# Index relu written in PSUM instead of SBUF, pieces of vector work on other engines, and the mixer's steps in another order

## The chip, the cores and the metric

The kernel runs on one core of one Trainium2 chip, with its inputs and its output in the chip's memory. The metric is the device time of one execution in microseconds (us), lower being better. Engines are called TensorE (PE in the profile), VectorE (DVE), ScalarE (ACT), GpSimd (POOL) and SyncE (SP, which here issues transfers).

## The reference

One decoder layer on 512 tokens of width 1024 in float32: a feed-forward block (FFN1), a token mixer, a second feed-forward block (FFN2). The mixer's group A selects keys with an indexer, then attends to them; group B is a latent attention over all earlier keys.

```python
x = x + 0.5 * swiglu(rmsnorm(x), gate1, up1, down1)          # D_FF = 2816
p = rmsnorm(x) @ W_in                                        # columns split among the groups
# group A, for each block i of 128 queries
idx_logits = einsum('bqhd,bsd->bqhs', q_idx, k_idx)          # 16 index heads of width 64
score = einsum('bqh,bqhs->bqs', w_idx, relu(idx_logits))
_, sel = top_k(where(causal, score, -inf), 128)              # 128 keys per query
att = softmax(q . k[sel]) @ v[sel]                           # 8 heads share one key and value
# group B: 8 heads, q and kv through normalised latents, dense causal softmax
x = x + concat(out_A, out_B) @ W_out
x = x + 0.5 * swiglu(rmsnorm(x), gate2, up2, down2)
```

## The kernel before

Every product of a projection is made in three matmuls of split operands (high times high, high times low, low times high; `mm3`, L137, L140 and L141). The split of a weight piece is a copy on ScalarE (L94) and a subtraction on VectorE or GpSimd (L95). FFN1 runs until 395 us of the span, the mixer until 691 us, then FFN2.

The mixer's order is a table, `ORDER`, of steps named by a letter and a number. `q` projects two index heads (24 matmuls of 384 columns), `s` rotates them and stacks their halves by four transfers, and `i` scores them (`index_heads`). `T`, `t`, `c`, `r`, `k`, `a`, `v`, `w` and `e` make the shared keys, values and weights of group A, `l` the five latents of group B (24 matmuls of 512 columns), `A`, `S`, `p`, `u`, `K`, `R`, `n` and `V` the remaining queries, keys and values. `b` takes that many rounds of the top-k: each finds eight maxima of the three score tiles and marks them as taken, 16 rounds and a last one, all on VectorE. After the bar stand the sixteen attention units: `g` gather, `s` score, `z` normalise, `a` apply, and `o` the output projection. In both tables all rounds of the top-k are complete before the first softmax. The order in which each engine gets its instructions is set when the program is built, from this table.

A second table, `ON_VECTOR`, names pieces of work that stand on VectorE; those not named stand on GpSimd, or on ScalarE for the copies `c`. `rT` and `rq` are the addition of a rotation, `mr...` its two multiplications (on GpSimd they need a copy of the projection by ScalarE first), `sq` and `sA` the subtraction of a stack, `w...` the subtraction of a weight split, `z` the scaling of one probability tile.

An index step `i` does two heads. Each head has three query blocks with score tiles of 256, 384 and 512 keys, so a step has six tiles. A tile is made by two matmuls (L707 with the keys' high part `kih`, L708 with the low part `kil`) into a PSUM tile `p`, a relu on ScalarE (L710) into `r`, and a VectorE operation (L711) that adds the weighted relu to the running score `idx`:

```python
r = fr()[:, :n]                       # fr: an SBUF pool of 4 buffers
nc.scalar.activation(r, p, AF.Relu)
nc.vector.scalar_tensor_tensor(out=score[i], in0=r, scalar=wt[:, i, h:h + 1], ...)
```

All PSUM tiles come from one pool of eight (`acc`, `sc` and `tr` are one function), which projections, index tiles, transposes and attention share in the order of the table.

Of the kernel before, what the change touches and what calls it, by code (L numbers as in the profile page):

```python
# [11 lines left out]
AF = mybir.ActivationFunctionType  # L12
# [3 lines left out]
T = 512  # L16
# [7 lines left out]
TAKEN = -3.0e38  # L24
TOPK = 128
BUFS = dict(pf=5, pr=4, ph=2, ah=7)
ORDER = """q0 q1 T c s0 r s1 t k q2 v w q3 i0 q4 a s2 i1 s4 q6 i2 q7 s3 q5 s6 s7 e s5 i3 l0 i4 i7 l1 i5 i6 l2 l3 l4 p b3 n0 u A0
A1 b2 K S0 A2 R b2 b2 S1 b2 A3 b3 S3 V S2 |
g0 s0 n1 g1 b2 g2 b2 s1 z0 s2 z1 b2 g3 g4 a0 s3 a1 b2 g5 z2 s4 a2 b2 z4 g6 z3 s5 g7 a3 s6 g8 z5 b2 b2 g9 a4 s7 g10 a5
b2 z6 s8 b2 a6 b2 b2 z7 a7 s9 o0 z8 g11 b2 b2 g12 b20 z9 b2 s10 z10 a8 s11 a9 a10 z11 g13 s12 o1 a11 g14 s13 z12 g15  # L30
s14 z13 s15 a12 z14 b2 o2 a13 a14 z15 a15 o3 o4 o5 b2 b2 o6 b2 o7 b2"""
ON_VECTOR = set("""c0.0 c0.1 c0.2 c0.3 c1.0 c1.2 c10.0 c11.0 c13.0 c14.3 c15.0 c15.1 c15.3 c2.1 c2.3 c3.1 c3.2 c3.3 c4.0 c4.3
c5.1 c6.0 c6.1 c6.2 c6.3 c7.2 gk5 gk7 kf mrA2 mrT mre mrq1 mrq2 mrq3 mrq5 mrq7 oa00 oa01 oa02 oa10 oa20 oa23
oa31 oa32 oa33 ob1 ob2 re rq1 rq2 rq3 rq5 ru1 sA2 sq6 sq7 su1 wA3 wV wl0 wl3 wo0 wo1 wo4 wo5 wo6 wo7 wq1 wq2
wq5 wq6 wq7 z0.0 z0.2 z0.3 z10.0 z10.2 z11.2 z12.0 z12.2 z12.3 z13.0 z13.2 z14.2 z14.3 z15.0 z15.1 z15.2 z2.3
z3.0 z3.1 z3.2 z3.3 z4.2 z4.3 z5.1 z5.2 z6.0 z6.2 z7.0 z7.1 z7.2 z7.3 z8.0 z9.0 z9.1""".split())

QA0, KA0, VA0, QI0, KI0, WI0, CQ0, CKV0, KR0 = 0, 512, 576, 640, 1664, 1728, 1744, 2128, 2384

# [355 lines left out]
def engine(nc, name):  # L395

    return nc.vector if name in ON_VECTOR else nc.gpsimd


def add_mixer_weights(k, w_in, w_uq, w_ukv, w_out):  # L400
# [163 lines left out]

    stream = [w for w in ORDER.split() if w in items]
    assert sorted(stream) == sorted(items)
# [7 lines left out]
def mixer(k, mp, mix, ids, xs, turn_rest, norm, tabs, g_q, g_kv, row_tile, out_done, on_token):  # L574
    nc = k.nc
# [3 lines left out]
    fr = lambda: pp.tile([P, T], F32, tag="r", name=k.name("r"), bufs=BUFS["pr"])  # L579
# [26 lines left out]

    steps = ORDER.split()
    begin = [ids[w] for w in steps if w in ("T", "q0", "q1", "t")][:2]
# [13 lines left out]
    def rope(p, tab, name, n0=0):  # L622
# [3 lines left out]
        nc.vector.tensor_tensor(out=a, in0=p, in1=c, op=ALU.mult)  # L626
        if "m" + name in ON_VECTOR:
            nc.vector.tensor_tensor(out=b[lower], in0=p[upper], in1=s[upper], op=ALU.mult)
# [32 lines left out]
    v = SimpleNamespace()  # L661
# [3 lines left out]
    wt = mp.tile([P, NT, 16], F32, tag="wt", name="wt", bufs=1)  # L665
    qst = lambda: mp.tile([P, T], F32R, tag="kf", name=k.name("qst"), bufs=8)
    score = {i: mp.tile([P, T], F32, tag="idx", name=f"idx_{i}", bufs=3)[:, :(i + 1) * P] for i in range(1, NT)}
# [24 lines left out]
    def rotary_key(x):  # L692
        scaled(tk, v.rows1)
        x = rope(x, tk, "re")
        h, l = f32r(), f32r()
        k.split(h, l, x, nc.gpsimd)
        for q, s in enumerate((h[0:16], h[64:80], l[0:16], l[64:80])):
            mv(kpe[16 * q:16 * q + 16, :], s)

    def index_heads(c, stacks):  # L700
        for j, s in enumerate(stacks):
            h = 2 * c + j
            for i in range(1, NT):
                n = (i + 1) * P
                p = k.sc()[:, :n]
                q = s[:, (i - 1) * P:i * P]
                nc.tensor.matmul(p, q, kih[:, :n], start=True, stop=False)  # L707
                nc.tensor.matmul(p, q, kil[:, :n], start=False, stop=True)  # L708
                r = fr()[:, :n]
                nc.scalar.activation(r, p, AF.Relu)  # L710
                nc.vector.scalar_tensor_tensor(out=score[i], in0=r, scalar=wt[:, i, h:h + 1],  # L711
                                               in1=cm(i) if h == 0 else score[i], op0=ALU.mult, op1=ALU.add)


# [33 lines left out]
    pq, pa, stacks, qf, qa, pe, vb, kf = {}, {}, {}, {}, {}, [], [], []  # L748
# [44 lines left out]
    def keys_b_out(j):  # L793
        v.scale_b = column(cols[0], 96.0 ** -0.5)
        rows = rows_of(k, cols[1], f32())
        for p in v.kpairs:
            x = mp.tile([P, T], F32, tag="kf", name=k.name("kf"), bufs=8)
            if "kf" in ON_VECTOR:
                nc.vector.tensor_tensor(out=x, in0=p, in1=rows, op=ALU.mult)
# [39 lines left out]
    def values_b(j):  # L839
        wv = k.weights(ids["V"])  # L840
        for j in range(NT):
            p = k.acc()
            for a in range(2):
# [5 lines left out]

    do = dict(T=keys, c=norm_column, t=rest, r=norm_rows, k=index_keys, a=attention_keys, v=rest_out, w=lambda j: values(v.x2),  # L850
              e=lambda j: rotary_key(v.x2), q=index_queries, s=index_stack, i=lambda j: index_heads(j, stacks.pop(j)), l=latent,
              K=keys_b, R=keys_b_out, p=rotary_b, u=rotary_b_out, n=nope, A=queries_a, S=stack_a, V=values_b, b=background)
    for w in steps[:steps.index("|")]:
# [29 lines left out]
    def normalise(n):  # L883
# [4 lines left out]
        for c, e in enumerate(out):  # L888
            if f"z{n}.{c}" not in ON_VECTOR:
                nc.gpsimd.tensor_tensor(out=e, in0=e, in1=rc[:, c:c + 1].to_broadcast(list(e.shape)), op=ALU.mult)  # L890
# [13 lines left out]
    def taken(u, j, to, p):  # L904
        if f"c{u}.{j}" in ON_VECTOR:
            nc.vector.tensor_copy(to, p)
        else:
            nc.scalar.activation(to, p, AF.Copy)
# [98 lines left out]
    def out_part(j):  # L1007
# [3 lines left out]
        for t in (2 * two, 2 * two + 1):  # L1011
            p = k.acc()
            for kt in range(4):
# [6 lines left out]
              a=lambda j: units[j].apply(), o=out_part, n=lambda j: k.weights(ids[f"n{j}"]), b=background)  # L1020
# [212 lines left out]
```

## Time and profile before

| what | value |
|---|---|
| median of 3 runs | 1060.78 us (1059.88 to 1061.4) |
| the profiled execution | 1061.52 us, its span 1059.7 us |
| mean granted TensorE clock | 0.987 |
| busy over the span | PE 1016.4 us (96%), DVE 513.2 (48%), ACT 384.3 (36%), POOL 147.5 (14%) |

The span is the time from the first to the last instruction that the profiler shows; 1.8 us of the profiled execution lie outside it. Busy times of the engines overlap, so they don't add up to the span. Clock 1.0 is TensorE at full speed. In a row of windows stand a stretch, its length, the busy time of each engine with its instructions, the granted clock, the share of the DMA engines' time and the rate of transfer. In a row of the timeline, a bracket gives the idle time ahead of the instruction and what ended it.

### The profile page before, as it was taken

The page shows a single profiled execution, that of the slowest core. Times are in us where ns is not written, and L with a number is a line of the kernel's source. Part 1 is how long each engine was busy: PE and PEld are TensorE (multiplying, and loading weights), DVE is VectorE, ACT ScalarE, POOL GpSimd, SP SyncE. Part 2 cuts the span into 40 slices and gives each one's busy share as a digit, 9 for nine tenths or more (in the row PEclk, how much of TensorE's full clock was granted, in tenths as well). Part 3 has the DMA queues.
Part 4 walks back from the last instruction along what each step waited for, and adds up shares of the span by engine and source line. Part 5 has one row for each costly group of instructions (what it writes and reads, how often), then busy time and mean ns, then how long its engine had stood idle before and what let it go on. Part 6 is the DMA issues. An engine that isn't in the chain of part 4 may idle for free.

```text
span 1059.7 us, 12214 instructions
## 1 busy us (share of the span) xinstructions
PE 1016.4 (96%) x4726; PEld 829.8 (78%) x4726; DVE 513.2 (48%) x897; ACT 384.3 (36%) x689; POOL 147.5 (14%) x142
## 2 busy tenths in 40 slices
PE   6999999999999999889879999999999999999997
PEld 4888888888888888768755567888888888888886
DVE  6433333233332346989996767553333233333343
ACT  5422222122222335563466556442222211222232
POOL 1000000000000026625975122000000000000000
PEclk9999999999999999989988999999999999999999
DMA  8322332233313123333350001344323232222302
GB/s 278 120 80 81 118 119 80 80 99 109 111 60 97 40 80 109 114 92 98 98 174 15 2 19 43 102 138 124 113 80 119 80 113 86 80 83 98 119 0 80
DMA packets 83390, 98.84 MB, mean 93 GB/s; under 512 B 9026, under 2 KB 65474, under 8 KB 83332
## 3 DMA queue, kind: packets, MB, share of 16 engines
q1 hardware_dynamic: 83328, 98.06, 29.4%
q8 instruction: 37, 0.61, 0.2%
q14 instruction: 21, 0.17, 0.1%
q10 hardware_dynamic: 4, 0.00, 0.0%
HBM read 91.89 MB, written 2.10 MB: 89 GB/s over the span
## 4 chain that ended last, share of the span: by engine, by line
PE 80%; DVE 12%; issue 3%; ACT 3%; POOL 1%; DMA 1%; SPq 0%; POOLq 0%; ACTq 0%; DVEq 0%
PE ps L137 24%; PE ps L140 24%; PE ps L141 24%; DVE idx L720 2%; DVE s L719 2%; DVE idx L711 1%; PE ps L960 1%; DVE wl L95 1%; PE ps L998 1%; DVE p L892 1%; PE ps L993 1%; PE ps L957 1%; DVE p L872 1%; PE ps L982 1%; DVE f L626 0%
## 5 line engine op out<-in xcount | busy, mean ns | idle before, releaser
L94 ACT ACTIVATE wh<-raw 128x1024 fp32r<-128x1024 f32 (+4 forms) x154 | 140.1, 925 | 381.1 <-PE ps L140 298.9
L95 DVE TENSOR_TENSOR wl<-raw,wh 128x1024 fp32r<-128x1024 f32 (+1 forms) x122 | 145.5, 1196 | 266.2 <-ACT wh L94 265.9
L137 PE MATMUL ps<-xh,wh 128*128 128x512 f32 (+2 forms) x712 | 265.9, 378 | 5.1 <-DVE res L1137 1.7
L141 PE MATMUL ps<-xh,wl 128*128 128x512 f32 (+2 forms) x712 | 267.3, 377 | 1.2 <-POOL wl L95 0.9
L140 PE MATMUL ps<-xh,wh 128*128 128x512 f32 (+2 forms) x712 | 267.2, 377 | 0.5 <-DVE xh L95 0.5
L137 PEld LDWEIGHTS ps<-xh,wh 128*128 128x128 f32 x712 | 133.7, 189 | 29.6 <-DVE f L629 2.1
L141 PEld LDWEIGHTS ps<-xh,wl 128*128 128x128 f32 x712 | 134.6, 189 | 24.9 <-POOL wl L95 1.3
L140 PEld LDWEIGHTS ps<-xh,wh 128*128 128x128 f32 x712 | 134.5, 189 | 23.6 <-DVE xh L95 0.7
L137 PE MATMUL ps<-wh,h 128*128 128x512 f32 x272 | 105.9, 389 | 0.0
L140 PE MATMUL ps<-wl,h 128*128 128x512 f32 x272 | 105.8, 389 | 0.0
L141 PE MATMUL ps<-wh,h 128*128 128x512 f32 x272 | 105.8, 389 | 0.0
L95 POOL TENSOR_TENSOR wl<-raw,wh 128x512 fp32r<-128x512 f32 (+5 forms) x32 | 43.3, 1374 | 394.4 <-ACT wh L94 389.8
L334 DVE TENSOR_TENSOR t<-ps,t 128x512 f32<-128x512 f32 x44 | 30.4, 691 | 138.5 <-PE ps L141 138.5
L94 ACT ACTIVATE w<-raw 128x1024 fp32r<-128x1024 f32 x32 | 33.9, 1061 | 117.5 <-PE ps L140 117.5
L137 PE MATMUL ps<-xh,w 128*128 128x512 f32 x176 | 68.5, 389 | 0.0
L141 PE MATMUL ps<-xh,w 128*128 128x512 f32 x176 | 68.5, 389 | 0.0
L140 PE MATMUL ps<-xh,w 128*128 128x512 f32 x176 | 68.5, 389 | 0.0
L289 POOL TENSOR_TENSOR fr<-tot,mhalf 128x1 f32<-128x1 f32 x12 | 7.0, 582 | 417.9 <-DVE tot L1180 360.1
L140 PEld LDWEIGHTS ps<-wl,h 128*128 128x128 f32 x272 | 51.1, 188 | 10.6
L141 PEld LDWEIGHTS ps<-wh,h 128*128 128x128 f32 x272 | 51.1, 188 | 10.6
L137 PEld LDWEIGHTS ps<-wh,h 128*128 128x128 f32 x272 | 51.0, 188 | 10.6
L95 DVE TENSOR_TENSOR w<-raw,w 128x1024 fp32r<-128x1024 f32 x32 | 39.2, 1225 | 29.8 <-ACT w L94 29.8
(214 smaller groups left out, 1346.2 us busy)
## 6 DMA issues: line engine op xcount, KB each, us to landing
raw<-in_w_up_dram SPq DMA_DIRECT2D x22, 1024.0 KB, 5.3
raw<-in_w_gate_dram SPq DMA_DIRECT2D x21, 1024.0 KB, 5.3
raw<-in_w_down_dram SPq DMA_DIRECT2D x20, 1024.0 KB, 5.0
raw<-in_w_in_dram SPq DMA_DIRECT2D x8, 1024.0 KB, 5.2
raw<-in_w_out_dram SPq DMA_DIRECT2D x4, 1024.0 KB, 5.8
res<-in_x_dram SPq DMA_DIRECT2D x4, 512.0 KB, 6.0
raw<-in_w_down_dram SPq DMA_DIRECT2D x4, 512.0 KB, 3.8
raw<-in_w_ukv_dram SPq DMA_DIRECT2D x2, 1024.0 KB, 4.9
```

What stands on the lines that cost most here:

```text
L94: i = self.nc.scalar.activation(hi, src, AF.Copy)
L95: (lo_engine or self.nc.vector).tensor_tensor(out=lo, in0=src, in1=hi.bitcast(F32), op=ALU.subtract)
L137: i = mm(out, wh, xh, start=first, stop=False)
L140: mm(out, wh, xl, start=False, stop=False)
L141: return i, mm(out, wl, xh, start=False, stop=last)
L334: nc.vector.tensor_tensor(out=u, in0=pu, in1=g, op=ALU.mult)
L711: nc.vector.scalar_tensor_tensor(out=score[i], in0=r, scalar=wt[:, i, h:h + 1], in1=cm(i) if h == 0 else score[i], op0=ALU.mult, op1=ALU.add)
L719: nc.vector.max(out=m8, in_=score[i])
L720: nc.vector.match_replace(out=score[i], in_to_replace=m8, in_values=score[i], imm_value=TAKEN)
L872: nc.vector.tensor_tensor_reduce(out=e, in0=p[:, :n], in1=bias, scale=1.0, scalar=-3.0e38, op0=ALU.add, op1=ALU.max, accum_out=mx[:, c:c + 1])
L892: nc.vector.tensor_scalar(out=e, in0=e, scalar1=rc[:, c:c + 1], scalar2=None, op0=ALU.mult)
L957: nc.tensor.transpose(p[:, i * P:(i + 1) * P], probs[i][:, j * P:(j + 1) * P], k.ident)
```

## The change

It has three parts. The relu of an index tile is written back into its own PSUM tile and VectorE reads that. Of the mixer's work ahead of the bar, eight pieces go from GpSimd to VectorE and two the other way; behind the bar fourteen scalings `z`, six copies `c` and two weight splits change engines. And `ORDER` has other places for `c`, `a`, `t`, `k`, `s2`, `l1`, `S1`, `n1` and some gathers, with the rounds of the top-k dealt out in smaller numbers. Lines of the changed kernel stand four or five lower than those of before.

```diff
-ORDER = """q0 q1 T c s0 r s1 t k q2 v w q3 i0 q4 a s2 i1 s4 q6 i2 q7 s3 q5 s6 s7 e s5 i3 l0 i4 i7 l1 i5 i6 l2 l3 l4 p b3 n0 u A0
...
+ORDER = """c q0 q1 T s0 r s1 t q2 v k w q3 s2 i0 a q4 i1 q6 i2 s4 q7 s3 q5 s6 s7 e s5 i3 l0 i4 l1 i7 i5 i6 l2 l3 l4 b1 p b1 n0 u
...
-                r = fr()[:, :n]
-                nc.scalar.activation(r, p, AF.Relu)
-                nc.vector.scalar_tensor_tensor(out=score[i], in0=r, scalar=wt[:, i, h:h + 1],
+                nc.scalar.activation(p, p, AF.Relu)
+                nc.vector.scalar_tensor_tensor(out=score[i], in0=p, scalar=wt[:, i, h:h + 1],
```

The names that leave `ON_VECTOR` are c0.2, c0.3, c6.2, c15.3, sq7, wl0, wo4, wo5, z3.1, z7.1, z8.0, z9.1, z12.0, z13.2, z15.1 and z15.2. Those that come in are c10.1, c15.2, mrq0, rT, sA0, sq0, sq2, sq3, wl2, wq0, z2.1, z4.0, z5.0, z8.1, z11.3 and z13.1 (and wl6, which names no piece).

On TensorE, the first index step stands in two halves: its six matmuls with `kih`, then matmuls of the next query projection (`ps<-xh,wh`), then the six with `kil`. Before, the second half began so:

```order
L140 MATMUL ps_2930<-xh_2629,wh_2811 128x384
L141 MATMUL ps_2930<-xh_2628,wl_2812 128x384
L708 MATMUL ps_2888<-kil,qst_2731 128x256
L708 MATMUL ps_2894<-kil,qst_2731 128x384
L708 MATMUL ps_2900<-kil,qst_2731 128x512
```

Now it begins so:

```order
L133 MATMUL ps_2944<-xh_2610,wh_2793 128x384
L136 MATMUL ps_2944<-xh_2611,wh_2793 128x384
L704 MATMUL ps_2902<-kil,qst_2729 128x256
L704 MATMUL ps_2907<-kil,qst_2729 128x384
L704 MATMUL ps_2912<-kil,qst_2729 128x512
```

The halves have 14 matmuls of the projection between them instead of 21; the other seven follow behind.

On TensorE, later, behind the last tiles of `i4`, step `i7` (`qst` is its stacked queries) followed at once before:

```order
L707 MATMUL ps_3343<-kih,qst_3022 128x512
L708 MATMUL ps_3343<-kil,qst_3022 128x512
L707 MATMUL ps_3349<-kih,qst_3198 128x256
L708 MATMUL ps_3349<-kil,qst_3198 128x256
L707 MATMUL ps_3355<-kih,qst_3198 128x384
```

Now the projection of latent `l1` stands there:

```order
L703 MATMUL ps_3312<-kih,qst_3069 128x512
L704 MATMUL ps_3312<-kil,qst_3069 128x512
L133 MATMUL ps_3321<-xh_2392,wh_3125 128x512
L136 MATMUL ps_3321<-xh_2393,wh_3125 128x512
L137 MATMUL ps_3321<-xh_2392,wl_3126 128x512
```

The 24 matmuls of `l1` have moved from behind `i7` to ahead of it.

On VectorE, the first accumulations of the index scores stood among a rotation (L626) and weight splits before:

```order
L711 SCALAR_TENSOR_TENSOR idx_2657<-r_2891,wt,cmask 128x256
L711 SCALAR_TENSOR_TENSOR idx_2658<-r_2897,wt,cmask 128x384
L711 SCALAR_TENSOR_TENSOR idx_2659<-r_2903,wt,cmask 128x512
L626 TENSOR_TENSOR f_3013<-ps_2930,tab_2644 128x384
L711 SCALAR_TENSOR_TENSOR idx_2657<-r_2909,wt,idx_2657 128x256
```

Now they read the PSUM tile, behind the subtraction of the stack `s2` (L645):

```order
L645 TENSOR_TENSOR h_2894<-f_2886,qst_2892 128x384
L91 TENSOR_TENSOR wl_2939<-raw_2853,wh_2938 128x8x64 x2
L706 SCALAR_TENSOR_TENSOR idx_2657<-ps_2902,wt,cmask 128x256
L706 SCALAR_TENSOR_TENSOR idx_2658<-ps_2907,wt,cmask 128x384
L706 SCALAR_TENSOR_TENSOR idx_2659<-ps_2912,wt,cmask 128x512
```

The input `r` in SBUF has become the PSUM tile `ps`, and the tile is free for another matmul only when VectorE has read it.

## Rows read from the trace of the kernel before

**Rows 1.** Windows: length, then busy PE, PEld, DVE, ACT, POOL; TensorE clock.

```profile
395.00:421.60 26.60, 24.75 (x124) 22.80 (x123) 15.84 (x27) 14.79 (x33) 18.04 (x18) 0.94 0.33 98
421.60:478.60 57.00, 49.34 (x238) 42.08 (x237) 53.85 (x73) 35.20 (x74) 23.96 (x16) 0.94 0.35 100
478.60:549.70 71.10, 63.83 (x298) 51.20 (x296) 71.04 (x175) 33.03 (x53) 56.15 (x46) 0.99 0.39 120
549.70:691.00 141.30, 130.88 (x661) 91.65 (x661) 97.57 (x284) 78.51 (x214) 36.26 (x42) 0.96 0.16 49
```

**Rows 2.** VectorE by shape, 395:479: count | busy us, mean ns | idle.

```profile
L711 DVE SCALAR_TENSOR_TENSOR idx<-r,wt,idx 128x512 f32<-128x512 f32 x15 | 14.8, 985 | 0.0
L711 DVE SCALAR_TENSOR_TENSOR idx<-r,wt,idx 128x384 f32<-128x384 f32 x15 | 11.9, 796 | 0.1
L711 DVE SCALAR_TENSOR_TENSOR idx<-r,wt,idx 128x256 f32<-128x256 f32 x15 | 10.0, 667 | 0.0
...
L742 DVE SCALAR_TENSOR_TENSOR lat<-ps,g_q_lat,lat 128x512 fp32r<-128x512 f32 x2 | 1.5, 747 | 2.0 <-ACT lat L741 2.0
...
L711 DVE SCALAR_TENSOR_TENSOR idx<-r,wt,cmask 128x512 f32<-128x512 f32 x1 | 0.7, 744 | 0.0
...
L711 DVE SCALAR_TENSOR_TENSOR idx<-r,wt,cmask 128x384 f32<-128x384 f32 x1 | 0.6, 611 | 0.0
...
L711 DVE SCALAR_TENSOR_TENSOR idx<-r,wt,cmask 128x256 f32<-128x256 f32 x1 | 0.5, 485 | 1.4 <-ACT r L710 1.4
```

**Rows 3.** Timeline of VectorE: start us, duration us, instruction.

```profile
432.51 0.74 DVE L711 SCALAR_TENSOR_TENSOR idx<-r,wt,idx 128x512 f32<-128x512 f32 x1
...
440.86 2.88 DVE L711 SCALAR_TENSOR_TENSOR idx<-r,wt,idx 128x512 f32<-128x512 f32 x1
...
454.16 0.55 DVE L649 TENSOR_TENSOR h<-f,qst 128x384 fp32r<-128x384 f32 x1
...
459.33 0.74 DVE L742 SCALAR_TENSOR_TENSOR lat<-ps,g_q_lat,lat 128x512 fp32r<-128x512 f32 x1
...
477.98 0.74 DVE L711 SCALAR_TENSOR_TENSOR idx<-r,wt,idx 128x512 f32<-128x512 f32 x1
```

**Rows 4.** Timeline of GpSimd: the same columns, at 440 and 459 us.

```profile
440.48 2.71 POOL L95 TENSOR_TENSOR wl<-raw,wh 128x1024 fp32r<-128x1024 f32 x1
...
458.93 1.62 POOL L95 TENSOR_TENSOR h<-f,h 128x512 fp32r<-128x512 f32 x1 [9.32 <-ACT lat L741]
```

**Rows 5.** Waits of VectorE, 395 to 551: us in total, times, longest.

```profile
DVE f L686 <- PE ps L683: 6.6, 1, 6.6
```

**Rows 6.** Waits of TensorE, 395 to 478: the same columns.

```profile
PE ps L707 <- DMA qst<-h: 4.0, 2, 3.0
PE ps L683 <- ACT f L775: 1.8, 1, 1.8
PE ps L137 <- DVE f L629: 1.6, 1, 1.6
PE ps L707 <- ACT r L710: 1.3, 2, 0.9
PE ps L707 <- DVE f L629: 0.5, 1, 0.5
```

**Rows 7.** Windows of TensorE alone: one 384-column projection, one index step.

```profile
425.24:429.43 4.19, 4.19 (x26) 1.00 0.83 258
429.43:431.57 2.14, 2.14 (x14) 1.00 0.45 155
```

**Rows 8.** Timeline of TensorE: its last index matmul of the last step.

```profile
471.92 0.40 PE L708 MATMUL ps<-kil,qst 128*128 128x512 f32 x1
```

**Rows 9.** ScalarE by shape, 385 to 690 us.

```profile
L710 ACT ACTIVATE r<-ps 128x512 f32<-128x512 f32 x16 | 9.7, 605 | 4.8 <-DVE idx L711 3.9 <-PE ps L708 0.8
```

**Rows 10.** Waits of ScalarE, 395 to 480 us.

```profile
ACT r L710 <- DVE idx L711: 9.5, 8, 3.3
```

**Rows 11.** GpSimd by shape, 550 to 691 us.

```profile
L890 POOL TENSOR_TENSOR p<-p,s 128x512 f32<-128x512 f32 x6 | 6.9, 1162 | 4.0 <-DVE s L887 3.1 <-PE ps L998 0.9
```

More of the change, by code (lines that the diff above doesn't have):

```diff
@@ L26 @@
 BUFS = dict(pf=5, pr=4, ph=2, ah=7)
-ORDER = """q0 q1 T c s0 r s1 t k q2 v w q3 i0 q4 a s2 i1 s4 q6 i2 q7 s3 q5 s6 s7 e s5 i3 l0 i4 i7 l1 i5 i6 l2 l3 l4 p b3 n0 u A0
[L28 to L36, printed above, removed]
+ORDER = """c q0 q1 T s0 r s1 t q2 v k w q3 s2 i0 a q4 i1 q6 i2 s4 q7 s3 q5 s6 s7 e s5 i3 l0 i4 l1 i7 i5 i6 l2 l3 l4 b1 p b1 n0 u
+A0 A1 b1 K S0 A2 b1 S1 R b5 A3 b2 S3 b2 V S2 b1 | g0 s0 g1 b2 g2 b1 s1 b1 n1 b1 z0 b1 s2 z1 b1 g3 b1 g4 a0 s3 b1 a1 g5
+z2 s4 a2 b3 z4 g6 z3 s5 b3 a3 b3 s6 g8 b1 z5 g9 g7 b1 a4 s7 b1 g10 b1 a5 z6 s8 b1 a6 b5 z7 g11 a7 z8 s9 b3 o0 b3 g12
+b2 s10 b4 z9 b4 z10 a8 s11 g13 a9 a10 z11 b1 s12 o1 a11 b1 g14 b1 s13 z12 s14 z13 g15 s15 a12 b1 z14 b1 o2 a14 a13 b1
+z15 a15 o3 o4 o5 b1 o6 b7 o7"""
+ON_VECTOR = set("""c0.0 c0.1 c1.0 c1.2 c10.0 c10.1 c11.0 c13.0 c14.3 c15.0 c15.1 c15.2 c2.1 c2.3 c3.1 c3.2 c3.3 c4.0 c4.3 c5.1 c6.0 c6.1 c6.3 c7.2 gk5 gk7 kf mrA2 mrT mre mrq0 mrq1 mrq2 mrq3 mrq5 mrq7 oa00 oa01 oa02 oa10 oa20 oa23 oa31 oa32 oa33 ob1 ob2 rT re rq1 rq2 rq3 rq5 ru1 sA0 sA2 sq0 sq2 sq3 sq6 su1 wA3 wV wl2 wl3 wl6 wo0 wo1 wo6 wo7 wq0 wq1 wq2 wq5 wq6 wq7 z0.0 z0.2 z0.3 z10.0 z10.2 z11.2 z11.3 z12.2 z12.3 z13.0 z13.1 z14.2 z14.3 z15.0 z2.1 z2.3 z3.0 z3.2 z3.3 z4.0 z4.2 z4.3 z5.0 z5.1 z5.2 z6.0 z6.2 z7.0 z7.2 z7.3 z8.1 z9.0""".split())
 QA0, KA0, VA0, QI0, KI0, WI0, CQ0, CKV0, KR0 = 0, 512, 576, 640, 1664, 1728, 1744, 2128, 2384
```

## The prediction

> **What bounds the kernel now.** I read the windows by stage first, then the waits of each engine in the mixer, then the groups by shape and single stretches of the timeline. In the front of the mixer (395 to 421.6 us, the end being the first index accumulation) no engine is full. In the index stage (421.6 to 478.6) VectorE is busy 53.85 of 57.00 us and TensorE 49.34. In the top-k stage (to 549.7, the first softmax) VectorE is busy 71.04 of 71.10, TensorE 63.83, GpSimd 56.15. In the attention stage (141.30 us) TensorE is busy 130.88, VectorE 97.57, GpSimd 36.26 [rows 1]. So from 421.6 to 549.7 VectorE sets the pace, and behind it TensorE. Both feed-forward blocks stay as they are.
>
> Within the index stage, VectorE's largest work is the accumulation L711. Its three shapes take 985, 796 and 667 ns on average, but the first head's, which differ only in one operand, take 744, 611 and 485 [rows 2]. The timeline tells why: the 128x512 one at 432.51 took 0.74 us, the one at 440.86 took 2.88, and a GpSimd subtraction ran from 440.48 to 443.19 over it [rows 3, 4]. Along the timeline, the L711 beside GpSimd work are stretched, the others not. An operation of the same kind that reads PSUM (L742, two of 747 ns) is not: at 459.33 it took 0.74 us inside a GpSimd subtraction that ran from 458.93 to 460.55 [rows 2 to 4]. ScalarE waited 9.5 us for L711 to free a buffer `r` [rows 10], so VectorE is late there, and its last accumulation starts at 477.98 and ends at 478.64, 6.3 us behind TensorE's last index matmul (471.92 + 0.40 = 472.32) [rows 3, 8].
>
> **The change part by part.** *The accumulation reads PSUM.* If it then behaves as L742 does, the stretch goes: 15 x (985 - 744) + 15 x (796 - 611) + 15 x (667 - 485) = 3.6 + 2.8 + 2.7 = 9.1 us of VectorE's time in the index stage [rows 2]. The ends are 0 (it stays stretched) and 9.1; I take 9.1, since L742 is the nearest row in operation, shape and neighbour. The relu that writes PSUM has no row. A cheaper one gains nothing, since ScalarE waits for others [rows 10], so the lower bound is 0; the upper is its 605 ns [rows 9] once more; 48 of them would be 29 us on an engine that is busy 35.20 of 57.00 us [rows 1], so that double would be felt, but the nearest row is the same relu into SBUF, and I take no difference.
>
> The first L742 gives the price of reading PSUM directly: 747 ns against 744 from SBUF, so nothing [rows 2]. [...]
>
> *The front.* TensorE's transposes L683 waited 1.8 us for ScalarE's copy of the projection (L775) [rows 6], and VectorE 6.6 us for those transposes [rows 5]. The copy is now issued ahead of the two copies that make `kih` and `kah`, so I remove 1.8. Then the first index step's second half stands behind 14 matmuls of the next projection instead of 21. A projection is 24 such matmuls in 4.19 us [rows 7], 0.175 each, so seven are 1.2 us. Together -3.0. VectorE takes on `rT`, `mrq0`, `sq0` and `sq2` here, at 0.55 us for a 384-wide piece [rows 3], some 2.9 us with two half-size products for `mrq0`; its 6.6 us of idle time covers them, and without that cover up to 2.9 would come on top. The least is -1.2 (the wait goes elsewhere); the most -4.6 (the granted clock is 0.94 over 26.6 us [rows 1], 1.6 us, if the pause that precedes the low stretch is what costs it).
>
> *The index stage by VectorE.* 57.00 - 9.1, plus `sq3` 0.55, less `sq7` 0.55, is a gain of 9.1; `wl2` for `wl0` is the same size. *By TensorE*, which has to deliver. Its waits here are 1.3 us for `r`, 4.0 for transferred stacks, 1.6 and 0.5 for rotations [rows 6]. The wait for `r` goes. The stacks came late because the subtractions before them stood on a stretched VectorE or on GpSimd; and `l1`'s 24 matmuls now stand ahead of `i7`, so TensorE has work while those transfers land. I take the 4.0 away and leave the 2.1. The seven moved matmuls come back here, +1.2. The stage also ends closer behind TensorE: the 6.3 us of lag can't fall below a relu and an accumulation (0.61 + 0.74 = 1.35 us [rows 2, 9]); at most eight tiles are outstanding (the pool), 8/6 of a head pair's 2 x (0.74 + 0.61 + 0.49) = 3.7, or 4.9 us. I take 3, a gain of 3.3. Sum by TensorE: -1.3 - 4.0 + 1.2 - 3.3 = -7.4. The smaller gain sets the end, and I take -7. Bounds: -3.4 if the stacks stay late, -9.1 by VectorE.
>
> No step moves a transfer past the weight loads' queue in number; each stack issues its four as before, at its step's new place.
>
> *The top-k stage.* VectorE is full, so what is added there is paid: `sA0`, a 512-wide subtraction, 0.75 by L742 [rows 2], bounds 0 and 1.5 (stretched to double). The rounds are dealt out differently, but all 16 still precede the softmax: 0. +0.7.
>
> *The attention stage.* VectorE sheds eight scalings and takes six, sheds two weight splits, and four copies more go to ScalarE than come back; GpSimd takes the rest in a stage where it is busy 36.26 of 141.30 us [rows 1]. TensorE sets this stage, so 0; GpSimd is the slower one at a scaling (1162 ns for 128x512 [rows 11]), and two of the last unit's lie behind the last score. Bounds +2.3 (two of these on the path) and -1.5 (two pieces of VectorE's 0.75 off it).
>
> **Sum.** -3.0 - 7.0 + 0.7 + 0 = -9.3 from the profiled execution's 1061.5 us, which is 0.7 above the median: 1052.2, and I say 1052.
>
> **The rivals.** *A, the gain doesn't pass the top-k stage.* When VectorE arrives earlier, TensorE (63.83 of 71.10 us) or GpSimd (56.15) would set the first softmax. Then only the front's 3.0 passes, and perhaps the 1.6 us that GpSimd loses with `sA0`: 1061.5 - 3.0 = 1058.5, or 1056.9. For it: TensorE's spare is only 7.3 us. Against it: both get their inputs earlier too, by the same shift.
>
> *B, slower: the PSUM tiles.* Before, ScalarE's relu freed a PSUM tile and four `r` buffers stood between it and VectorE; now VectorE frees it. An index step's six tiles and a projection's fill nearly all of eight, so a step's first tile has to wait for the accumulations of the step before. Behind the waiting matmul stand all later matmuls, projections too, so TensorE can't make up. If VectorE is a whole step behind, the seven later steps wait for about half of its 3.7 us each, 7 x 1.85 = 13 us, and the end is 1061.5 - 9.3 + 13 = 1065. It decides when VectorE's lag at a step's start passes 3.7 us. For it: at 429.43 the third step's first matmul began [rows 7] while VectorE's accumulations of the second ran until 432.51 + 0.74 = 433.25 [rows 3], a lag of 3.8. Against it: that lag holds stretched accumulations, a quarter of L711's 36.7 us [rows 2], and a projection of 4.19 us stands between steps. [...]
>
> *C, the change doesn't do what it says.* The accumulation stays stretched with a PSUM source. Then the front's 3.0 stays, less 0.7 and what the banks cost (1.3 us, the wait for `r` doubled): 1060 to 1061. Against it: L742.
>
> *D, the PSUM source has a fixed price.* It takes 7 / 48 = 0.15 us more per accumulation to eat the index gain; a third of that gives 1055. Against it: 747 against 744.
>
> **How the numbers follow.** Forecast 0.62, A 0.18, B 0.10, C 0.06, D 0.04. No change is what lies within 0.2%, about 2.1 us. Forecast, D and two thirds of A are faster: 0.62 + 0.04 + 0.12 = 0.78. C and a third of A are the same: 0.12. B is slower: 0.10. The sum of the bounds is -4.6 - 9.1 + 0 - 1.5 = -15.2, or 1046.3, and -1.2 - 3.4 + 1.5 + 2.3 = -0.8, or 1060.7. I leave out the outermost on either side and B: 1047 to 1060.
>
> **What the profile will show.** The three shapes of the accumulation at about 750, 610 and 490 ns, also where GpSimd works; the wait of L683 gone and the first accumulation near 418.6; the index stage some 50 us long, with VectorE no longer near full in it; the first softmax near 540.5; an attention stage of the same length. Wrong would be: accumulations as long as before (C); waits of TensorE's index matmuls for the accumulations, over 1 us at several steps (B); VectorE idle ahead of the first softmax, with TensorE or GpSimd as what it waits for (A).

## The result and the profile after

The changed kernel takes 1053.62 us (median of 6 runs, 1052.84 to 1054.13) against 1060.67 for the kernel before (6 runs): a ratio of 0.9934, 95% interval 0.9921 to 0.9947. It is faster by 7.0 us. The profiled execution, 1052.84 us with a span of 1051.0, is the fastest of the six.

The trace after is cut at the events of [rows 1], with two put more exactly: FFN1 ends with its last residual addition on VectorE (382.56 us; 383.06 before, not 395), and attention with TensorE's last output projection (680.86; 689.55 before, not 691). The first view is the windows of the changed kernel, with the same columns as [rows 1].

```profile
382.56:418.47 35.91, 35.84 (x201) 33.25 (x199) 27.36 (x44) 19.51 (x42) 15.62 (x16) 1.00 0.41 129
418.47:467.06 48.59, 45.88 (x221) 37.79 (x222) 44.55 (x75) 31.29 (x68) 22.04 (x15) 1.00 0.40 120
467.06:538.01 70.95, 65.91 (x310) 54.72 (x308) 70.59 (x176) 33.70 (x55) 54.33 (x44) 0.98 0.39 118
538.01:680.86 142.85, 131.85 (x659) 92.76 (x659) 94.58 (x276) 78.36 (x214) 44.73 (x47) 0.93 0.15 46
```

Cut the same way, the stages before are 38.54, 57.12, 71.03 and 139.80 us. The front is 2.6 us shorter, the index stage 8.5, the top-k stage the same, and attention 3.0 us longer; FFN1 ended 0.5 earlier. These make the 8.7 us between the two spans.

VectorE's groups by shape in the mixer answer to [rows 2]: the index accumulations now read PSUM.

```profile
L706 DVE SCALAR_TENSOR_TENSOR idx<-ps,wt,idx 128x512 f32<-128x512 f32 x15 | 11.2, 744 | 0.3 <-ACT ps L705 0.3
L706 DVE SCALAR_TENSOR_TENSOR idx<-ps,wt,idx 128x384 f32<-128x384 f32 x15 | 9.2, 610 | 0.0
L706 DVE SCALAR_TENSOR_TENSOR idx<-ps,wt,idx 128x256 f32<-128x256 f32 x15 | 7.2, 478 | 1.1 <-ACT ps L705 1.1
```

They were 985, 796 and 667 ns. All 48 take 29.3 us instead of 38.6. TensorE's waits in the index stage answer to [rows 6]:

```profile
PE ps L703 <- DVE idx L706: 2.4, 5, 1.0
PE ps L133 <- ACT f L628: 0.3, 1, 0.3
```

The waits for the transferred stacks (4.0 us), for `r` (1.3) and for the rotations (2.1) are gone; 2.4 us of a new one have come, for VectorE to read a PSUM tile. VectorE's last accumulation ends 3.5 us behind TensorE's last index matmul (467.06 against 463.51), where it was 6.4 (478.72 against 472.32).

Attention lost time at one place. The timelines of VectorE, GpSimd and TensorE near 566 us show it (the first row groups six scalings in a row, the second is the third of them alone).

```profile
565.11 6.89 DVE L887 TENSOR_SCALAR p<-p,s 128x128 f32<-128x128 f32 x6
...
566.48 2.58 DVE L887 TENSOR_SCALAR p<-p,s 128x512 f32<-128x512 f32 x1
```

```profile
566.30 2.47 POOL L91 TENSOR_TENSOR wl<-raw,wh 128x1024 fp32r<-128x1024 f32 x1
```

```profile
570.40 0.84 PE L952 MATMUL ps<-ident,p 128*128 128x128 f32 x6 [2.21 <-DVE p L887]
572.05 0.77 PE L952 MATMUL ps<-ident,p 128*128 128x128 f32 x4 [0.80 <-DVE p L887]
```

A 128x512 scaling took 2.58 us while GpSimd subtracted over it (0.47 at 545.68 in the same profile, where GpSimd is idle beside it), and TensorE's transposes waited for the scalings. This is the stretch of the accumulations once more, on another operation. It isn't new, only longer: before, six scalings stood in a row there too. They and one of them (VectorE, then GpSimd):

```profile
577.31 5.72 DVE L892 TENSOR_SCALAR p<-p,s 128x384 f32<-128x384 f32 x6
...
579.11 2.52 DVE L892 TENSOR_SCALAR p<-p,s 128x384 f32<-128x384 f32 x1
```

```profile
579.00 2.42 POOL L95 TENSOR_TENSOR wl<-raw,wh 128x1024 fp32r<-128x1024 f32 x1 [0.56 <-ACT wh L94]
```

Before, the subtraction waited for its copy on ScalarE and met the fifth scaling; now it waits for nothing and meets the third. TensorE's waits for scalings in the whole stage rose from 2.2 to 4.3 us.

### The profile page after: what moved, and what is told of

Same layout as the page of the kernel before. It is cut to its first block, busy times and chain, and to the rows that moved or that the text cites. A ratio compares the mean times of both kernels' runs of the same rounds, so it can differ in the third digit from the quotient of the medians.

```text
span 1051.0 us, 12201 instructions
## 1 busy us (share of the span) xinstructions
PE 1015.8 (97%) x4726; PEld 829.9 (79%) x4726; DVE 508.1 (48%) x899; ACT 382.6 (36%) x690; POOL 144.5 (14%) x138
## 4 chain that ended last, share of the span: by engine, by line
PE 82%; DVE 6%; POOL 3%; ACT 3%; issue 2%; DMA 2%; SPq 1%; POOLq 0%; DVEq 0%; ACTq 0%
PE ps L133 25%; PE ps L136 25%; PE ps L137 25%; PE ps L955 2%; DVE p L887 1%; DMA raw<-in_w_in_dram 1%; PE ps L993 1%; POOL wl L91 1%; DVE wl L91 1%; PE ps L988 1%; PE ps L952 1%; DVE p L867 1%; SPq L635 1%; ACT ps L705 1%; DMA xh<-kpe 1%
## 5 line engine op out<-in xcount | busy, mean ns | idle before, releaser
L91 DVE TENSOR_TENSOR wl<-raw,wh 128x1024 fp32r<-128x1024 f32 (+1 forms) x122 | 142.6, 1174 | 266.1 <-ACT wh L90 265.7
L91 DVE TENSOR_TENSOR w<-raw,w 128x1024 fp32r<-128x1024 f32 x32 | 39.2, 1225 | 29.8 <-ACT w L90 29.8
```

The costliest lines, as they stand in the source:

```text
L91: (lo_engine or self.nc.vector).tensor_tensor(out=lo, in0=src, in1=hi.bitcast(F32), op=ALU.subtract)
```

## The experiments

Two tables give the kernels at once; b2, b3 and b4, of one run each, stand with their experiments. The ratio is to the kernel before on the same chip; the stages, each row from one profiled execution, are measured between the events named above.

| kernel | median us | ratio, 95% interval |
|---|---|---|
| changed kernel | 1053.62 | 0.9934 [0.9921, 0.9947] |
| a1: relu back in SBUF | 1060.32 | 1.0005 [0.9994, 1.0015] |
| b1: kernel before, relu in PSUM | 1054.48 | 0.9948 [0.9935, 0.9961] |
| a2: attention's pieces back | 1053.12 | 0.9931 [0.9918, 0.9943] |
| a3: order back | 1056.84 | 0.9966 [0.9954, 0.9978] |
| a4: pieces ahead of the bar back | 1056.17 | 0.9954 [0.9939, 0.9968] |
| a6: six PSUM tiles | 1086.03 | 1.0236 [1.0222, 1.0251] |
| a7: new up to the bar, old behind | 1052.70 | 0.9917 [0.9904, 0.9931] |
| a8: six scalings on ScalarE | 1053.82 | 0.9936 [0.9924, 0.9948] |
| a9: a7 with one weight split on VectorE | 1047.16 | 0.9881 [0.9865, 0.9898] |

| kernel | front | index | top-k | attention |
|---|---|---|---|---|
| before | 38.54 | 57.12 | 71.03 | 139.80 |
| changed | 35.91 | 48.59 | 70.95 | 142.85 |
| a1 | 35.87 | 56.06 | 72.45 | 142.83 |
| b1 | 37.14 | 50.74 | 71.39 | 139.13 |
| a2 | 35.92 | 48.27 | 70.96 | 141.42 |
| a3 | 35.86 | 51.07 | 72.97 | 141.88 |
| a4 | 39.93 | 48.34 | 70.93 | 143.06 |
| a6 | 38.77 | 65.71 | 68.22 | 153.19 |
| a7 | 35.76 | 48.63 | 70.94 | 141.94 |
| a8 | 35.96 | 48.55 | 70.96 | 143.77 |
| a9 | 35.92 | 48.33 | 70.95 | 136.57 |

FFN1 ends between 382.56 and 384.55 us from one execution to the next, so the stages, not the spans, are to be compared, with TensorE's clock beside them: a stretch at half clock (granted 0.50, as from 411.1 to 414.5 us before) stands in some of these executions and not in others.

### a1 and b1: the relu alone, and all but the relu

a1 undoes the first part of the change in the changed kernel:

```diff
-                nc.scalar.activation(p, p, AF.Relu)
-                nc.vector.scalar_tensor_tensor(out=score[i], in0=p, ...
+                r = fr()[:, :n]
+                nc.scalar.activation(r, p, AF.Relu)
+                nc.vector.scalar_tensor_tensor(out=score[i], in0=r, ...
```

> The changed kernel with the relu back in an SBUF buffer; pieces and order stay changed. Theory 1 (the accumulations gain because an accumulation that reads PSUM is not stretched by GpSimd's work): the stretch comes back, mean of the 128x512 shape near 950 ns instead of 744, the index stage 5 to 9 us longer than the 48.5 of the changed kernel, the time 1057 to 1062. Rival 1 (the gain comes from the order and the pieces, the relu's place matters little): index stage within 1.5 us of 48.5, time 1053 to 1055.

b1 makes only this edit, the other way round, in the kernel before.

> The kernel before with the relu in PSUM alone. Theory 1: accumulations of 744, 610 and 478 ns, VectorE's work in the index stage 9 us less; but the old order and pieces keep the first accumulation near 421.6 and TensorE waits for PSUM tiles; index stage 50 to 53 us, time 1054 to 1058. Rival 1: no faster than before, 1059 to 1062. Rival 2 (PSUM tiles freed by VectorE hold TensorE up unless the order is changed with them): waits of TensorE's index matmuls for VectorE of over 6 us, time over 1061.

The relu's place is worth nearly all: alone it gives 5.8 us (1054.48 against 1060.29 for before), and without it order and pieces give nothing (1.0005). In a1 the accumulations take 39.2 us again and the index stage 56.06; TensorE's waits there show that the stacks' transfers are late again:

```profile
PE ps L703 <- DMA qst<-h: 6.2, 1, 6.2
PE ps L703 <- ACT r L706: 1.2, 1, 1.2
```

So a late VectorE made those transfers late, as the prediction had it, and `l1`'s new place, which a1 keeps, did not cover them. In b1 TensorE waits 2.8 us for PSUM tiles, far from rival 2's 6.

### b2, b3 and b4: is it GpSimd that stretches them?

b2 adds two GpSimd additions of 128x256 ahead of each index head in the kernel before, b3 the same in b1 (the sums are thrown away), and b4 memsets in b2's place:

```diff
         for j, s in enumerate(stacks):
+            junk = pp.tile([P, 256], F32, tag="junk", name=k.name("junk"), bufs=1)
+            nc.gpsimd.tensor_tensor(out=junk, in0=ta[0][:, :256], in1=ta[1][:, :256], op=ALU.add)
+            nc.gpsimd.tensor_tensor(out=junk, in0=ta[0][:, :256], in1=ta[1][:, :256], op=ALU.add)
```

> The kernel before, its relu in SBUF, with two more GpSimd additions of 128x256 (both inputs and the output in SBUF, the sums not used) ahead of each index head's tiles. Theory 1: more of the accumulations lie beside GpSimd work and are stretched; mean of the 128x512 shape well over 985 ns (1100 to 1700), VectorE's accumulations 45 us or more in all instead of 38.6. Rival 1: the long accumulations of before have another cause; the means stay within 5%.

> The same additions in the kernel before with the relu in PSUM. Theory 1: accumulations of 744, 610 and 478 ns still, 29.3 us in all, even with GpSimd busy for most of the index stage. Rival: with a GpSimd kept busy they are stretched too, and a PSUM source only lessens it.

> As with the added additions in the kernel before, but memsets of 128x256 in their place, which write SBUF and read nothing. If GpSimd's reading is what stretches an accumulation: accumulations beside a memset keep 744, 610 and 478 ns, and the sum stays near 38.6 us. If any GpSimd work does: means over 1100 ns for the 128x512 shape.

VectorE's groups by shape, of b2 and then of b3:

```profile
L715 DVE SCALAR_TENSOR_TENSOR idx<-r,wt,idx 128x384 f32<-128x384 f32 x15 | 14.1, 943 | 0.0
L715 DVE SCALAR_TENSOR_TENSOR idx<-r,wt,idx 128x512 f32<-128x512 f32 x15 | 13.6, 906 | 0.0
L715 DVE SCALAR_TENSOR_TENSOR idx<-r,wt,idx 128x256 f32<-128x256 f32 x15 | 11.7, 778 | 0.0
```

```profile
L714 DVE SCALAR_TENSOR_TENSOR idx<-ps,wt,idx 128x512 f32<-128x512 f32 x15 | 11.1, 739 | 0.0
L714 DVE SCALAR_TENSOR_TENSOR idx<-ps,wt,idx 128x384 f32<-128x384 f32 x15 | 9.1, 606 | 0.0
L714 DVE SCALAR_TENSOR_TENSOR idx<-ps,wt,idx 128x256 f32<-128x256 f32 x15 | 7.1, 472 | 0.0
```

The size forecast for b2 was too high: 41.6 us in all where 45 or more were forecast, and the 128x512 shape fell to 906 ns, probably because the new additions moved GpSimd's long operations to other neighbours. The split by neighbour is clear, though. Worked out from start and end of each instruction in the timelines: in b2 the 22 accumulations that lie beside GpSimd work take 1.04, 1.32 and 1.15 us on average (256, 384 and 512 columns), the 26 others 0.476, 0.610 and 0.742. In b3, 29 lie beside it and take 0.471, 0.605 and 0.740; the 19 others 0.473, 0.608 and 0.739. With a PSUM source the neighbour made no difference. b2 took 1070.1 us and b3 1062.96, a single run of each. That b3 is so much longer than b1 is not the accumulations' doing: its front is 40.3 us and its index stage 57.3, and beside 2.5 us for PSUM tiles TensorE waits there for a weight split, a copy and a rotation (1.3, 1.2 and 0.7 us).

b4 (1061.27 us, one run) tells nothing: the memsets, which wait for nothing, ran between 385 and 413 us, before the first accumulation. Whether GpSimd work that only writes stretches one stays open.

### a3 and a4: order and pieces

a3 is the changed kernel with the `ORDER` of before, a4 with the ten pieces ahead of the bar as before (of `ON_VECTOR` only the names that differ are printed, here and below):

```diff
-ORDER = """c q0 q1 T s0 r s1 t q2 v k w q3 s2 i0 a q4 i1 ...
+ORDER = """q0 q1 T c s0 r s1 t k q2 v w q3 i0 q4 a s2 i1 ...
```

```diff
-ON_VECTOR: mrq0 rT sA0 sq0 sq2 sq3 wl2 wq0
+ON_VECTOR: sq7 wl0
```

> The changed kernel with the order of before; relu in PSUM and pieces stay changed. By the prediction's terms the order gives the 1.8 us wait of the transposes, 1.2 us from the seven matmuls, and the work that covers the stacks' transfers, and costs nothing behind the bar: time 1056 to 1060. If the order costs the attention its 3 us, the attention stage is back at 141 to 142 us and the time is 1052 to 1056.

> The changed kernel (relu in PSUM, new order), with the ten pieces ahead of the bar back on their engines of before. The prediction gave the front's gain to the order. If so: the front, from the end of the first feed-forward block to the first accumulation, is 36 us as in the changed kernel (38.5 before), and the time 1053 to 1055. If the pieces make it (the kernel with the old order and the new pieces has 35.9): front 37 to 38.5 us, time 1054 to 1057.

The front's gain comes with the pieces. With the old order and the new pieces it is 35.86 us, with the new order and the old pieces 39.93, more than either forecast. Before, the front ended with TensorE: VectorE stood idle 1.4 us for the relu of the first tile [rows 2]. In the changed kernel that relu ends at 417.22, and VectorE, busy with weight splits, takes the tile 1.25 us later, without idle time before it. In a3 it has none there either. VectorE and ScalarE in the changed kernel:

```profile
417.26 1.29 DVE L91 TENSOR_TENSOR wl<-raw,wh 128x512 fp32r<-128x512 f32 x2
418.47 0.48 DVE L706 SCALAR_TENSOR_TENSOR idx<-ps,wt,cmask 128x256 f32<-128x256 f32 x1
```

```profile
416.86 0.36 ACT L705 ACTIVATE ps<-ps 128x256 f32<-128x256 f32 x1
```

So in a3 the transposes' wait, 2.7 us, doesn't lengthen the front. But it isn't free. The windows of a3's front and index stage:

```profile
382.76:418.62 35.86, 33.13 (x177) 30.64 (x176) 26.63 (x43) 17.98 (x38) 15.55 (x16) 0.95 0.42 129
418.62:469.70 51.08, 48.63 (x245) 41.75 (x244) 45.06 (x76) 33.14 (x72) 21.58 (x15) 1.00 0.39 114
```

In the same front TensorE does 177 matmuls instead of 201, and the 24 that are missing, as many as one projection of 4.19 us [rows 7], are left for the index stage: 245 instead of 221. This reading of the counts was not tried by a run of its own.

In a4 TensorE waits for the index keys instead (waits of TensorE, 383 to 420 us):

```profile
PE ps L703 <- ACT kih L671: 2.0, 1, 2.0
PE ps L679 <- ACT f L770: 0.8, 1, 0.8
```

`kih` is copied from the rotated keys, whose addition (`rT`) is on GpSimd in a4. That this piece, of the ten, is the cause is argued, not tried. The order's part lies in the index stage and behind it: 51.07 and 72.97 us in a3 against 48.59 and 70.95.

b1, with neither order nor pieces, has a front 1.4 us shorter than before. That is TensorE's clock. The windows of the two fronts, before and b1:

```profile
383.06:421.60 38.54, 36.69 (x197) 34.11 (x196) 22.46 (x39) 18.54 (x40) 20.89 (x21) 0.96 0.39 123
383.55:420.69 37.14, 35.29 (x198) 32.71 (x197) 22.43 (x38) 18.70 (x40) 20.90 (x21) 1.00 0.40 128
```

The wait of 1.8 us is in both; behind it the clock fell to half from 411.1 to 414.5 before, and not in b1. The profiled execution of b1 has a mean clock of 0.991, its five others 0.987 or 0.988, so this may belong to that execution and not to the kernel.

### a6: how near the PSUM tiles are

```diff
-        return self.ps("ps", 8)
+        return self.ps("ps", 6)
```

> The changed kernel with six PSUM tiles in the pool instead of eight (everything else the same). It measures rival B of the prediction, that TensorE waits for tiles which VectorE frees: the changed kernel's index matmuls wait 2.4 us in all. With two tiles fewer, by B's working, every later step waits for most of the step before: waits of 6 to 13 us in the index stage, and more in the attention, time 1060 to 1075. If tiles are no limit: waits below 4 us, time below 1056.

Two tiles fewer cost 32 us against the changed kernel, more than forecast, 17.1 of them in the index stage. Waits of TensorE there (422.29 to 488.00 us):

```profile
PE ps L703 <- DVE idx L706: 6.5, 4, 2.6
PE ps L703 <- DVE f L625: 3.3, 1, 3.3
PE ps L133 <- DVE idx L706: 0.9, 1, 0.9
PE ps L703 <- ACT f L628: 0.9, 1, 0.9
```

The waits for accumulations are 7.4 us, within the forecast's 6 to 13; beside them stand 4.2 us of other waits and a clock of 0.90 in this stage instead of 1.00. So rival B's mechanism is real; with eight tiles it cost 2.4 us of waits. Seven were not tried.

### a2, a7, a8 and a9: what attention lost

a2 is the changed kernel with the scalings, copies and weight splits of the attention as before; a7 also has the order of before behind the bar. a2's edit, of which a7 has the same:

```diff
-ON_VECTOR: c10.1 c15.2 z2.1 z4.0 z5.0 z8.1 z11.3 z13.1
+ON_VECTOR: c0.2 c0.3 c6.2 c15.3 wo4 wo5 z3.1 z7.1 z8.0 z9.1 z12.0 z13.2 z15.1 z15.2
```

> The changed kernel with the attention's scalings, copies and weight splits on the engines of before. Theory 2 (the attention stage is 3 us longer in the changed kernel because six scalings in a row on VectorE at 565 hold TensorE's transposes up and its clock falls behind the wait): the wait at 568 to 570 goes, the stage is 141 to 142.5 us instead of 144.3, the time 1051 to 1052. Rival 3 (the order behind the bar, or the earlier arrival of the softmax, costs it): stage still 144, time 1053 to 1055.

> The changed kernel up to the bar (order, pieces, relu in PSUM), with the order and the pieces of before behind the bar. Theory 2 as it now stands (either the new order or the new pieces behind the bar puts a run of scalings ahead of a transpose that TensorE waits for, 4.3 to 4.7 us against 2.2): both gone, that wait is back at about 2.2, the attention stage at 139 to 140 us, the time 1049 to 1051. Rival 3 (the attention stage is longer because it starts earlier, with its transfers and splits not ready): stage 142 us or more, time 1052.5 to 1054.

a2 refuted the first form of the theory: its stage, 141.42, lay in the forecast's range, but the wait for the scalings was still 4.7 us. The old order alone (a3) left it at 4.6. a7 refuted the second form, for its stage was 141.94, though behind the bar its tables are those of b1 with 139.13. In a7 six scalings again stand in a row beside the same subtraction. Timelines of VectorE and then of GpSimd in a7:

```profile
567.05 6.79 DVE L887 TENSOR_SCALAR p<-p,s 128x384 f32<-128x384 f32 x6
...
568.39 2.38 DVE L887 TENSOR_SCALAR p<-p,s 128x128 f32<-128x128 f32 x1
```

```profile
568.14 2.54 POOL L91 TENSOR_TENSOR wl<-raw,wh 128x1024 fp32r<-128x1024 f32 x1
```

A 128x128 scaling, 0.28 us where GpSimd is idle (at 578.65 us before), took 2.38. In b1 the same subtraction waited 0.55 us for its copy, as before, and began later (571.40, 1.7 us behind the first scaling instead of 1.1), and the six took 5.72. Stage and time of a7 are close to what its rival 3 forecast, but what differs at this place is an input that was ready earlier, not one that was late. So what attention costs depends on what meets there, and a shift of half a microsecond seems to be enough.

a8 takes the six off VectorE in the changed kernel:

```diff
-            if f"z{n}.{c}" not in ON_VECTOR:
+            if f"z{n}.{c}" in ['z3.0', 'z3.2', 'z3.3', 'z4.0', 'z4.2', 'z4.3']:
+                nc.scalar.activation(e, e, AF.Copy, scale=rc[:, c:c + 1])
+            elif f"z{n}.{c}" not in ON_VECTOR:
```

> The changed kernel with the scalings z3.0, z3.2, z3.3, z4.0, z4.2 and z4.3 on ScalarE (a copy with a scale) instead of VectorE. Theory 2, third form (these six took 6.87 us in a row on VectorE because GpSimd's subtractions stretch them, as they stretched the accumulations; TensorE waits 3.0 us for them and runs at half clock for 7 us behind): the waits at 568 to 572 fall below 1 us, the low stretch of the clock goes, attention stage 138.5 to 140.5 us instead of 142.9, time 1049.5 to 1052. Rival: ScalarE's own work behind them (splits of the next heads, copies) is late instead, stage 142 us or more, time 1053 to 1056.

The waits at 568 to 572 went, but the rival held: a copy of the transposes stood behind the six on ScalarE, and TensorE waited for that. ScalarE, then TensorE, in a8:

```profile
566.46 2.93 ACT L885 ACTIVATE p<-p,s 128x128 f32<-128x128 f32 x6
```

```profile
574.69 1.11 PE L957 MATMUL ps<-h,xh 128*64 128x512 f32 x1 [3.90 <-ACT h L905]
```

a9 leaves the scalings and moves their neighbour: it is a7 with one name more, so that this subtraction stands on VectorE, at 567.70 behind the six, where it takes 1.73 us.

```diff
+ON_VECTOR: wo2
```

> The kernel a7 (new up to the bar, old behind it) with the weight split wo2 on VectorE instead of GpSimd, where it stands behind the six scalings. Theory 2, third form (GpSimd's 128x1024 subtraction at 568.1, 2.54 us, stretches the scalings beside it, and this is what the attention stage of a7 lost against the 139.1 us of the kernel with the relu alone): no scaling is over 1.6 us long, the six take 4.0 to 5.8 us instead of 6.8, TensorE's wait for scalings in the stage is 2.5 to 4 us instead of 4.7, the stage 139.5 to 141 instead of 141.9, time 1050.5 to 1052. Rival: GpSimd's next splits move up and stretch them as much, stage within 0.6 us of 141.9, time 1052 to 1053.5.

Windows of a9's attention, its six scalings, what GpSimd does there, and TensorE's wait for scalings:

```profile
538.13:674.71 136.58, 129.14 (x662) 90.84 (x660) 95.46 (x283) 77.66 (x212) 36.19 (x42) 0.96 0.16 48
```

```profile
564.63 2.60 DVE L887 TENSOR_SCALAR p<-p,s 128x384 f32<-128x384 f32 x6
```

```profile
564.67 1.08 POOL L885 TENSOR_TENSOR p<-p,s 128x128 f32<-128x128 f32 x2 [4.41 <-PE ps L938]
566.81 1.53 POOL L91 TENSOR_TENSOR st<-qf,st 64x512 fp32r<-64x512 f32 x1 [1.06 <-ACT st L90]
```

```profile
PE ps L952 <- DVE p L887: 1.3, 1, 1.3
```

The six fell from 6.79 to 2.60 us, the wait from 4.7 to 1.3, the stage from 141.94 to 136.57: the theory's third form holds, with more gain than it forecast (a stage of 139.5 to 141), for GpSimd's next split waited 1.06 us for its copy and met only the last scaling, which took 0.48. a9's stage is also 3.2 us shorter than that of the kernel before, which had the stretch too. a9 is the fastest kernel, 13.2 us below the kernel before on its chip (1047.16 against 1060.38) and, by the ratios, 0.5% below the changed one.

## Why the prediction held, and where it didn't

- **The accumulation in PSUM**: right in mechanism and size. 9.1 us of VectorE's time were forecast, 38.6 - 29.3 = 9.3 measured. A PSUM source cost nothing more: 744, 610 and 478 ns against 744, 611 and 485 undisturbed from SBUF. So rivals C and D fall.
- **The index stage**: -8.5 us against the -7 taken, within the bounds of -3.4 and -9.1. The waits for `r` and for the stacks went as taken, the stacks' by the relu alone (a1 has 6.2 us of it, b1 and a3 none). The lag fell by 2.9 (3.3 taken). The waits for rotations (2.1), which were left in, went too. Rival B's waits for PSUM tiles (2.4), for which the sum had no term, came. The 1.2 us of the seven matmuls did not: TensorE had done 201 at the first accumulation, four more than before, not seven fewer. And the sum had no term for TensorE's clock, which was 0.94 in this stage before and 1.00 after. Before, it was at half from 455.5 us on, in the longest wait for a stack:

```profile
455.50:462.30 6.80, 4.02 (x12) 3.46 (x13) 6.04 (x9) 5.01 (x11) 2.69 (x2) 0.50 0.32 70
```

The twelve matmuls of an index step took TensorE 4.02 us there and 2.14 at full clock [rows 7], so some 1.9 us went to the clock.
- **The front**: right in size (-2.6 us against -3.0; that the first accumulation came at 418.47, with 418.6 forecast, is helped by FFN1's ending 0.5 earlier), wrong in what sets it. The steps that failed are "The copy is now issued ahead ... so I remove 1.8" and the seven matmuls, as terms of the front. TensorE's wait did go, but the front now ends with VectorE: a3 keeps the wait and has the same front, a4 has the new order and a longer one. What the order saves TensorE shows a stage later, by the counts of matmuls in a3. VectorE's work in the front rose by 4.9 us (22.46 to 27.36), not by 2.9; the prediction has no term for `wq0`, which goes to VectorE too. Which of the pieces make the front was not tried.
- **The top-k stage**: 0.1 us shorter instead of 0.7 longer. VectorE is full there as before (70.59 of 70.95), but has 0.4 us less to do; the term for `sA0` was not separated from what else moved. Rival A didn't happen: the whole shift of 11.7 us reached the first softmax (538.01 against 549.75).
- **Attention**: 0 was forecast, +3.0 came, beyond the bound of +2.3. The step that failed is "TensorE sets this stage, so 0". It set the stage on the average, but at one place six scalings on VectorE did, stretched by GpSimd as the accumulations had been: TensorE waited there 0.85 us before and 3.0 after, and behind that its clock was at half from 572.5 to 579.3. The prediction had this mechanism in hand and applied it to one operation, though in the trace of before six scalings already took 5.72 us there. (Its count of the copies is wrong as well: four go to ScalarE and two come back, so two more, not four. Nothing was summed from it.)
- **The sum**: -9.3 forecast, -8.7 in the profiled spans, -7.0 in the medians, since the two profiled executions lie on different sides of their medians. That the sum came so near is in part luck: the three stages ahead of attention and FFN1's end gave 11.7 us instead of 9.3, and attention took 3.0 of that back.

## What to carry to other kernels

Where VectorE paces a stage, compare one shape's mean with its undisturbed duration; if the long ones lie beside GpSimd work, give them a PSUM source or move the neighbour (each was tried here on one operation), and look for every other operation that shares the disturbance. Price a piece that is moved by what then runs beside it, not by its own duration: one 1.7 us subtraction in another place was worth 5.4 us of the stage here. And where a wait goes, look at TensorE's clock too, before and after (0.94 and 1.00 in the index stage here). A stage that is bound by one engine on the average can still be set by another at the one place where a wait stands: here TensorE, busy 131.85 of the attention's 142.85 us, waited 3.0 us for VectorE's six scalings.

## What was not expected of the hardware

A scaling with one SBUF input (`p<-p,s`, 128x128) took 2.38 us beside a GpSimd subtraction against 0.28 alone (before, at 578.65), while the accumulation with one SBUF input and one in PSUM was untouched (0.740 against 0.739 us in b3). How long the scaling takes seems to be set by the subtraction: in a7 the scaling ends at 570.77 and the subtraction at 570.68, and in the changed kernel the 128x512 one ends at 569.06 and the subtraction at 568.77. What tells the two operations apart was not tried: no run gives the scaling a PSUM source.

TensorE's clock fell behind the 3.0 us of waits for scalings: it was 0.50 from 572.5 to 579.3 us in the changed kernel. The granted clock of the whole attention stage is 0.93 there, and 0.96 before and in a9. TensorE's busy time for about as many matmuls (659 to 662) is 131.9 us in the changed kernel, 130.4 before and 129.1 in a9.
